# Feed-forward modulation of features 1024 to 2047 loaded beside gate and up chunks that start on half the features

## The chip, the cores and the metric

One core of a Trainium2 chip runs the whole program. The metric is device time in microseconds (us), from one launch, the smaller the better. TensorE (PE in the rows) does the matmuls and their weight loads (PEld), VectorE (DVE) and ScalarE (ACT) the element-wise work, SyncE (SP) issues every DMA of the kernel, GpSimd (POOL) is nearly unused. All inputs are float32. A product of two matrices is made of three matmuls in a rounded float32 format: each operand is split into a rounded part and a residue, and the product of the two residues is left out.

## The reference, cut to what matters

One encoder block over 256 tokens of 2048 features. A vector `c` gives six rows of 2048 numbers; two of them shift and scale the input of the mixer, two that of the feed-forward part, and two gate what is added to `x`.

```python
mod = (silu(c) @ ada_w + ada_b)                      # 2048 x 12288
shift_a, scale_a, gate_a, shift_f, scale_f, gate_f = split(mod, 6)
h = rmsnorm(x, norm1_w) * (1 + scale_a) + shift_a
proj = h @ w_in                                      # retention and attention heads
x = x + gate_a * (concat(retention, attention) @ w_o)
h = rmsnorm(x, norm2_w) * (1 + scale_f) + shift_f
ff = (silu(h @ w_gate) * (h @ w_up)) @ w_down        # 2048 -> 5632 -> 2048
x = x + gate_f * ff
return rmsnorm(x, final_norm_w)
```

## The kernel before

**Weights.** All weights lie in one stream in HBM, in the order in which they are used, and each is read once. A weight step loads 512 KB (two k-tiles of 128 features by 512 columns) into one of six staging buffers (`stg`). ScalarE casts it to the rounded part (`whi`, three buffers), VectorE subtracts to get the residue (`wlo`, three buffers), and TensorE does 12 matmuls of 512 columns for it: 2 k-tiles, 2 blocks of 128 tokens, 3 products. `run` walks a list of steps and keeps up to LOOK = 3 loads ahead of the step whose matmuls it records, except ahead of the steps named in URGENT.

**Modulation sets.** `ada_set` computes 512 columns of one of the six rows: eight loads of 512 KB (units), and at the end a spread that adds the bias. Units run in one of two ways. On TensorE a unit is four matmuls with the vector as a 32-column stationary operand (`c_pad`); four of them share the array side by side. On VectorE it is two multiply-adds of 128x512 into `ada_acc`. A 1 in a string of digits puts the set on TensorE. SC_F and SH_F are the scale and shift of the feed-forward part, GT_A and GT_F the two gates.

**Stages.** First the mixer's input projection, then attention and retention heads, the output projection, the norm of the new `x` (`norm_x2`), and the feed-forward part: eleven chunks of 512 columns of gate and up (`gate_up`), packed into the stationary layout by `pack`, and four chunks of `down`. Retention has, head by head, scores on TensorE (L615), a decayed copy on VectorE (`rP`, L618), an output on TensorE (L626), and statistics on VectorE; weight steps of `w_in` and `w_o` are filled in between by FILL_R. From attention on, the modulation sets GT_A, SC_F and SH_F are put between these steps at a rate set by ADA_RATE, in this order: four of GT_A, then SC_F and SH_F for features below K_LATE x 128 = 1536. By ADA_PE2 the second set of GT_A, the third of SC_F and the first of SH_F are on TensorE. One set of GT_F is on TensorE too, and fills the wait at the norm.

**Start of the feed-forward part.** The input of it (`h2`) is built two k-tiles at a time by `build_h2`. Chunks g0, u0 and g1 (gate 0, up 0, gate 1) first run over the six pairs of k-tiles below K_LATE, a weight step of each in turn: 18 weight steps. Beside each of them stands one unit of SC_F or SH_F for the last four k-tiles, 16 in all, on VectorE. Then the last k-tiles of `h2` are built and the three chunks are finished. The remaining three sets of GT_F follow on VectorE, one unit in every five weight steps.

The order in which each engine gets its instructions is set by a scheduler in the language layer, and each engine then runs its own list in that order. The lines that the steps below speak of are L122 (load), L124 (cast), L126 (residue), L132 to L134 (the three matmuls), L185 (load of a unit), L196 and L198 to L200 (a unit on TensorE and on VectorE), L222 (spread) and L728 (the norm's broadcast).

Of the kernel before, what the change touches and what calls it, by code (L numbers as in the profile page):

```python
# [8 lines left out]
F32 = mybir.dt.float32  # L9
# [32 lines left out]
LEAD = [1, 1, 3, 3, 3, 3, 3]  # L42
ADA_PE2 = "010000110000"
ADA_RATE = 0.8
# [41 lines left out]
def encoder_block(ctx: ExitStack, tc: tile.TileContext, x, cols, rows, pos, stream, out):  # L86
# [24 lines left out]
    c_act = const.tile([P, KT], F32, name="c_act")  # L111
    c_pad = const.tile([P, KT, 32], F32, name="c_pad")

# [59 lines left out]

    def ada_set(pool, sec, k0, nk, rowdst, on_pe):
        n = nk * P
# [4 lines left out]
        def acc_tile():  # L180
            return (pool or late["pool"]).tile([P, n], F32, name="ada_acc", tag="ada_acc", bufs=2 if pool else 1, padded_shape=[P, 512])

# [53 lines left out]

    def ada_stream(pool, sets):

        units, late = [], []
        for st in sets:  # L240
            loads, ends = ada_set(pool, *st)
# [10 lines left out]
    mid = mid_cm.__enter__()  # L252


# [115 lines left out]
    steps = [f(norm_x)]  # L370
    for u in ada_stream(mid, [(SC_A, *GROUPS[0], None, True), (SH_A, *GROUPS[0], None, True)]):
        steps += u
    steps += [f(turn_x, 0), f(build_h1, 0)]
    for gi, (k0, nk) in enumerate(GROUPS[:-1]):
        g0, gn_ = GROUPS[gi + 1]
        units = ada_stream(mid, [
            (sec, k, min(4, g0 + gn_ - k), None, ADA_PE[2 * gi + i] == "1") for k in range(g0, g0 + gn_, 4) for i, sec in enumerate((SC_A, SH_A))
# [290 lines left out]
    x2 = {}  # L668
    x2T = [pacc[n].rearrange("p b (k t) -> p (b k) t", t=T) for n in "vg"]

# [38 lines left out]

    def turn_x2(n):  # L710
        for g in range(2):
# [19 lines left out]
    h2 = {}  # L731

    def build_h2(k):
# [56 lines left out]
    early += [(sec, k, min(4, K_LATE - k), None) for sec in (SC_F, SH_F) for k in range(0, K_LATE, 4)]  # L790
    units = ada_stream(mid, [(*st, on == "1") for st, on in zip(early, ADA_PE2)])
    pe = dma = 0.0
# [17 lines left out]

    fill_f = [ada_set(mid, GT_F, 4 * i, 4, lambda: late["gate_f"], True) for i in range(N_FILL)]
    loads = [u for loads, _ in fill_f for u in loads]
    steps += [f(gate_f_tile)] + loads[:F_LEAD] + [f(turn_x2, 3)] + loads[F_LEAD:F_LEAD + F_MORE] + [f(norm_x2)] + loads[F_LEAD + F_MORE:]
    ends_f = [y for _, ends in fill_f for y in ends]


    def ffn_tiles():
        mid_cm.__exit__(None, None, None)
        late["pool"] = ctx.enter_context(tc.tile_pool(name="ffn", bufs=1))
        late["ap"] = late["pool"].tile([P, FT, 2 * T], F32R, name="ap")  # L820

    def sg_tile():
        late["sg"] = big.tile([P, 2, NB, CH], F32, name="sgs", tag="m8")

    def pack(j):
        for g in range(2):
            b = pairs(bank())
            ap = late["ap"]
# [3 lines left out]
            ks = slice(4 * j + 2 * g, 4 * j + 2 * g + 2)  # L832
            S.copy(ap[:, ks, 0:T], b)
            V.tensor_tensor(ap[:, ks, T:2 * T], b, ap[:, ks, 0:T].bitcast(F32), op=ALU.subtract)  # L834

    def gate_up(j, name, w):
        st = {}

        def body(kp, whi, wlo):
# [16 lines left out]
        return [("w", (w, kp, 2, j * CH, CH), lambda hi, lo, kp=kp: body(kp, hi, lo)) for kp in range(0, KT, 2)]  # L856

    units = ada_stream(None, [(GT_F, 4 * i, 4, lambda: late["gate_f"], False) for i in range(N_FILL, 4)])
    n_ch = DFF // CH
    g0, u0, g1, u1 = [gate_up(j, n, w) for j in range(2) for n, w in (("g", "w_gate"), ("u", "w_up"))]  # L860
    h_late = [(sec, K_LATE, KT - K_LATE, None) for sec in (SC_F, SH_F) if K_LATE < KT]
    units_h = ada_stream(mid, [(*st, on == "1") for st, on in zip(h_late, ADA_PE3)])
    steps.append(f(build_h2, 0))
    for kp in range(0, K_LATE, 2):
        if kp + 2 < K_LATE:
            steps.append(f(build_h2, kp + 2))
        for w in (g0, u0, g1):
            steps.append(w[kp // 2])
            if w is (g0, u0, g1)[F_END]:
                steps += ends_f  # L870
                ends_f = []
            for _ in range(H_RATE):
                if units_h:
                    steps += units_h.pop(0)
    for u in units_h:
        steps += u
    for k in range(K_LATE, KT, 2):
        steps.append(f(build_h2, k))
    steps += [f(ffn_tiles), f(sg_tile)]
    for w in (g0, u0, g1):  # L880
        steps += w[K_LATE // 2:]
    for j in range(1, n_ch):
        ws = u1 if j == 1 else gate_up(j, "g", "w_gate") + gate_up(j, "u", "w_up")
# [14 lines left out]
    def down(n):  # L898
# [14 lines left out]
        def body(kp, whi, wlo):  # L913
# [6 lines left out]
            for tb in range(NB):  # L920
                for q, hi, lo in st["w"]:
                    for i in range(2):
                        mm_tokens(st["o"][tb], late["ap"], q + i, tb, hi[:, i], lo[:, i], q + i == 0, q + i == FT - 1)
                if kp == FT - 2:
# [68 lines left out]
```

## Time and profile before

| | us |
|---|---|
| median of 3 runs | 1264.54 |
| lowest and highest run | 1262.27 and 1264.93 |
| the profiled execution, time | 1266.85 |
| the profiled execution, span of its core | 1264.9 |
| TensorE busy | 1224.4 |
| VectorE busy | 843.6 |
| ScalarE busy | 599.7 |
| bytes moved | 315.28 MB |

The span runs from the first to the last instruction of the core; the profiled execution's time is 1.95 us more than its span. Its mean granted TensorE clock is 0.992 of full speed. Matmul records overlap, since a matmul is recorded until its last result is out, so a TensorE that is busy the whole time may still not issue at its peak; the distance from one matmul's start to the next tells that.

### The profile page before, as it was taken

Reading aid. Unit: us, or ns where it says so; the run is one execution under the profiler, and the core shown is the slowest. Engines: PE = TensorE matmul, PEld = TensorE weight load, DVE = VectorE, ACT = ScalarE, POOL = GpSimd, SP = SyncE. Lnnn points to the kernel's source line nnn. Section 1 sums busy time; section 2 is a strip of 40 time slices with the busy share of each in tenths; the row PEclk is TensorE's granted clock in tenths of the full one; section 3 lists DMA queues with packets and bytes.
Section 4 is the critical chain, followed back from the end, with each engine's and each line's share of the span. In section 5 each row is a group of like instructions: output and inputs, shape, how many; then the busy total and the mean of one; then the engine's idle time right before and its main releaser. Section 6 shows DMA issues by size and latency. Waiting matters only on the chain.

```text
span 1264.9 us, 16232 instructions
## 1 busy us (share of the span) xinstructions
PE 1224.4 (97%) x6022; PEld 971.6 (77%) x6022; DVE 843.6 (67%) x1185; ACT 599.7 (47%) x811; POOL 1.7 (0%) x9
## 2 busy tenths in 40 slices
PE   5899899999999999899999999999999999999997
PEld 2676667788787788578888888888888888888885
DVE  2596988879997998886655556655654454554544
ACT  4552454645556665646344444444444434444433
POOL 0000000000000000000000000000000000000000
PEclk9999999999999999999999999999999999999998
DMA  8888898888877887897667657665765655555552
GB/s 337 321 301 309 276 317 299 290 311 290 298 255 289 306 301 278 299 349 250 211 220 233 201 183 274 222 203 202 275 219 188 226 187 194 190 198 190 192 196 88
DMA packets 88799, 315.28 MB, mean 249 GB/s; under 512 B 10248, under 2 KB 10376, under 8 KB 88208
## 3 DMA queue, kind: packets, MB, share of 16 engines
q1 hardware_dynamic: 88720, 314.24, 72.0%
q8 instruction: 47, 0.77, 0.3%
q14 instruction: 32, 0.26, 0.1%
HBM read 312.11 MB, written 2.10 MB: 248 GB/s over the span
## 4 chain that ended last, share of the span: by engine, by line
PE 85%; DVE 5%; DMA 5%; ACT 2%; issue 1%; SPq 0%; ACTq 0%; DVEq 0%
PE bank L133 25%; PE bank L134 25%; PE bank L132 25%; DMA stg<-in_stream 5%; DVE wlo L126 2%; PE bank L148 2%; PE bank L196 2%; DVE ada_acc L200 1%; ACT whi L124 1%; PE bank L514 1%; PE bank L138 1%; PE bank L513 1%; PE bank L626 1%; PE bank L615 1%; PE bank L140 1%
## 5 line engine op out<-in xcount | busy, mean ns | idle before, releaser
L126 DVE TENSOR_TENSOR wlo<-stg,whi 128x1024 fp32r<-128x1024 f32 (+2 forms) x400 | 478.7, 1198 | 341.2 <-ACT whi L124 339.6
L124 ACT CAST whi<-stg 128x1024 fp32r<-128x1024 f32 (+2 forms) x400 | 412.8, 1033 | 532.3 <-PE bank L134 417.2
L132 PE MATMUL bank<-whi,actt 128*128 128x512 f32 (+1 forms) x1184 | 457.9, 393 | 11.7 <-ACT whi L124 8.4
L133 PE MATMUL bank<-wlo,actt 128*128 128x512 f32 (+1 forms) x1184 | 461.7, 390 | 7.4 <-DVE wlo L126 7.0
L134 PE MATMUL bank<-whi,actt 128*128 128x512 f32 (+1 forms) x1184 | 459.2, 388 | 0.3 <-DVE actt L145 0.3
L132 PEld LDWEIGHTS bank<-whi,actt 128*128 128x128 f32 x1184 | 222.0, 189 | 64.9 <-ACT whi L124 12.7
L133 PEld LDWEIGHTS bank<-wlo,actt 128*128 128x128 f32 x1184 | 223.7, 189 | 62.4 <-DVE wlo L126 17.0
L134 PEld LDWEIGHTS bank<-whi,actt 128*128 128x128 f32 x1184 | 223.7, 189 | 44.9 <-DVE actt L145 1.1
L200 DVE SCALAR_TENSOR_TENSOR ada_acc<-stg,c_act,ada_acc 128x512 f32<-128x512 f32 (+1 forms) x240 | 175.0, 730 | 15.8 <-DMA stg<-in_stream 12.8
L132 PE MATMUL bank<-whi,ap 128*128 128x512 f32 x352 | 137.0, 389 | 0.0
L134 PE MATMUL bank<-whi,ap 128*128 128x512 f32 x352 | 136.9, 389 | 0.0
L133 PE MATMUL bank<-wlo,ap 128*128 128x512 f32 x352 | 136.9, 389 | 0.0
L133 PEld LDWEIGHTS bank<-wlo,ap 128*128 128x128 f32 x352 | 66.1, 188 | 13.8
L132 PEld LDWEIGHTS bank<-whi,ap 128*128 128x128 f32 x352 | 66.1, 188 | 13.8
L134 PEld LDWEIGHTS bank<-whi,ap 128*128 128x128 f32 x352 | 66.1, 188 | 13.5
L196 PE MATMUL bank<-stg,c_pad 128*32 128x256 f32 x544 | 48.0, 415 | 11.1 <-DMA stg<-in_stream 11.0
L196 PEld LDWEIGHTS bank<-stg,c_pad 128*32 128x32 f32 x544 | 13.0, 112 | 35.2 <-issue 26.0
L852 ACT ACTIVATE sgs<-bank 128x512 f32<-128x512 f32 x22 | 13.1, 597 | 10.5 <-PE bank L134 9.8
L145 DVE TENSOR_TENSOR actt<-hfull,actt 128x256 fp32r<-128x256 f32 x40 | 16.3, 420 | 2.2 <-ACT actt L144 2.1
L854 DVE TENSOR_TENSOR sgs<-bank,sgs 128x512 f32<-128x512 f32 x22 | 14.3, 682 | 0.6 <-PE bank L134 0.6
L834 DVE TENSOR_TENSOR ap<-bank,ap 128x512 fp32r<-128x512 f32 x22 | 14.1, 681 | 0.0
L226 DVE TENSOR_REDUCE mod<-bank 128x4 f32<-128x512 f32 (+3 forms) x18 | 8.0, 442 | 8.5 <-PE bank L222 8.3
(222 smaller groups left out, 711.1 us busy)
## 6 DMA issues: line engine op xcount, KB each, us to landing
stg<-in_stream SPq DMA_DIRECT2D x568, 512.0 KB, 4.4
stg<-in_stream SPq DMA_DIRECT2D x16, 288.0 KB, 4.1
stg<-in_stream SPq DMA_DIRECT2D x8, 384.0 KB, 2.8
xt<-in_x SPq DMA_DIRECT2D x2, 1024.0 KB
acc_cq<-in_x SPq DMA_DIRECT2D x8, 256.0 KB
out<-x SPq DMA_DIRECT2D x8, 256.0 KB, 2.9
acc_k<-in_rows SPq DMA_DIRECT2D x1, 1024.0 KB, 7.7
fw<-in_rows SPq DMA_DIRECT2D x1, 1024.0 KB
```

The costliest lines, as they stand in the source:

```text
L124: S.copy(hi, stg)
L126: V.tensor_tensor(lo, stg, hi.bitcast(F32), op=ALU.subtract)
L132: PE.matmul(o, lhsT=ah, rhs=whi, start=first, stop=False)
L133: PE.matmul(o, lhsT=ah, rhs=wlo, start=False, stop=False)
L134: PE.matmul(o, lhsT=al, rhs=whi, start=False, stop=last)
L145: V.tensor_tensor(dst[:, k, T:2 * T], tmp, dst[:, k, 0:T].bitcast(F32), op=ALU.subtract)
L148: PE.transpose(b[:, j, tb * P:(tb + 1) * P], src, ident)
L196: PE.matmul(a[q:q + 32, c:c + wide], lhsT=c_pad[:, k], rhs=w[:, j], start=c == 0 and k < 4, stop=c + wide == n and k >= KT - 4)
L200: V.scalar_tensor_tensor(out=a, in0=w[:, j], scalar=c_act[:, k:k + 1], in1=a, op0=ALU.mult, op1=ALU.add)
L834: V.tensor_tensor(ap[:, ks, T:2 * T], b, ap[:, ks, 0:T].bitcast(F32), op=ALU.subtract)
L852: S.activation(sg, o[tb], AF.Silu)
L854: V.tensor_tensor(sg, o[tb], sg, op=ALU.mult)
```

## The change

K_LATE goes from 12 to 8: the part of SC_F and SH_F that is ready ahead of the feed-forward part ends at feature 1024. Ahead of it stand 8 sets in place of 10, and of these only the second set of GT_A is on TensorE. The set that fills the wait at the norm is the third of SC_F (`h_late[0]`) in place of the first of GT_F. The other three late sets (24 units) run on VectorE beside the first 36 weight steps of the feed-forward part: g0, u0 and g1 over four pairs of k-tiles, and then gate chunks 2 to 7 over the same four pairs. Gates 1 to 7 leave PSUM after that half: ScalarE copies their two banks to SBUF (`spill`), and at the end of the second half VectorE adds the copy back. All four sets of GT_F follow on VectorE, one unit in every three weight steps.

Buffers move with it: the upper half of `x2T` and the temporary of `build_h2` (which now takes a `stg` buffer) leave the pool that is closed early, and `ap` becomes one tile for each chunk. The matmuls of a gate or up step go block by block instead of k-tile by k-tile; their number is the same.

```diff
-ADA_PE2 = "010000110000"
+ADA_PE2 = "01000000"
...
-N_FILL = 1
...
-K_LATE = 12
-ADA_PE3 = "00"
-H_RATE = 1
+K_LATE = 8
+N_SPILL = 7
...
     def build_h2(k):
...
-        V.tensor_tensor(v, v, rstd_b.unsqueeze(1).broadcast_to([P, 2, T]), op=ALU.mult)
+        if k < K_LATE:
+            scale_x2(k, 2)
         for j in range(2):
-            tmp = mid.tile([P, T], F32, name="hfull", tag="hfull", bufs=2)
+            tmp = wp.tile([P, T], F32, name="hfull", tag="stg", bufs=6)
...
-            if kp == 0:
+            if kp == 0 or (spilled and kp == K_LATE):
                 st["o"] = [bank() for _ in range(NB)]
             o = st["o"]
-            for i in range(2):
-                k = kp + i
-                for tb in range(NB):
-                    mm_tokens(o[tb], h2[k // 4], k % 4, tb, whi[:, i], wlo[:, i], k == 0, k == KT - 1)
+            for tb in range(NB):
+                for i in range(2):
+                    k = kp + i
...
-                if name == "g":
+                if name == "g" and (j, tb) in spills:
+                    V.tensor_tensor(sg, o[tb], spills.pop((j, tb)), op=ALU.add)
+                    S.activation(sg, sg, AF.Silu)
...
+        def spill(kp, whi, wlo):
+            body(kp, whi, wlo)
+            if kp < K_LATE - 2:
+                return
+            if j % 2:
+                spills["t"] = late["pool"].tile([P, 4, 2 * T], F32, name="spilled", tag="ap", bufs=n_ch)
+            for tb in range(NB):
+                d = spills["t"][:, 2 - 2 * (j % 2) + tb]
+                S.copy(d, st["o"][tb])
+                spills[j, tb] = d
...
+    def half_step(w):
+        nonlocal count
+        steps.append(w)
+        count += 1
+        if count % 4 and units_h:
+            steps.extend(units_h.pop(0))
...
+    for j in range(2, N_SPILL + 1):
+        for w in gs[j][:half]:
+            half_step(w)
     for u in units_h:
         steps += u
...
-            if i % 5 == 4 and units:
+            if i % 3 == 2 and units:
                 steps += units.pop(0)
```

The first place is retention on VectorE. Before, between two residues of `w_in` or `w_o` steps, only retention's own instructions stand there (`rP` the decayed scores, `bs` and `gnst` statistics, `dec` the decays):

```order
L618 SCALAR_TENSOR_TENSOR rP_3816<-bank_3813,dec_3809 128x256 x2
L629 BN_STATS bs_3835<-bank_3830 128x6
L629 BN_STATS bs_3838<-bank_3830 128x6
L630 BN_AGGR gnst_110<-bs_3835 128x2
L611 SCALAR_TENSOR_TENSOR dec_3872<-dist_108,lg_109,dec_3872 128x384
L630 BN_AGGR gnst_110<-bs_3838 128x2
L610 TENSOR_SCALAR dec_3928<-dist_108,lg_109 128x384
L611 SCALAR_TENSOR_TENSOR dec_3928<-dist_108,lg_109,dec_3928 128x384
L126 TENSOR_TENSOR wlo_3828<-stg_3824,whi_3826 128x1024
```

In the changed kernel, the piece that leads to a residue of the same stage:

```order
L627 BN_STATS bs_3766<-bank_3761 128x6
L616 SCALAR_TENSOR_TENSOR rP_3750<-bank_3747,dec_3743 128x256 x2
L628 BN_AGGR gnst_110<-bs_3766 128x2
L627 BN_STATS bs_3769<-bank_3761 128x6
L197 SCALAR_TENSOR_TENSOR ada_acc_3601<-stg_3709,c_act_80,ada_acc_3601 128x512
L628 BN_AGGR gnst_110<-bs_3769 128x2
L608 TENSOR_SCALAR dec_3793<-dist_108,lg_109 128x384
L609 SCALAR_TENSOR_TENSOR dec_3793<-dist_108,lg_109,dec_3793 128x384
L195 TENSOR_SCALAR ada_acc_3803<-stg_3741,c_act_80 128x512
L123 TENSOR_TENSOR wlo_3810<-stg_3806,whi_3808 128x1024
```

Multiply-adds into `ada_acc` of the two SH_F sets now stand on VectorE between retention's steps.

The second place is the same stretch on TensorE, where `rout` and `att` are turned and the scores (`qT`, `kT`) are made. Before:

```order
L148 MATMUL bank<-ident,rout 128x128 x8
L196 MATMUL bank<-stg,c_pad 32x256 x4
L148 MATMUL bank<-ident,att 128x128 x8
L196 MATMUL bank<-stg,c_pad 32x256 x4
L615 MATMUL bank<-qT,kT 128x256 x2
L196 MATMUL bank<-stg,c_pad 32x256 x4
L626 MATMUL bank<-acc_v,rP 128x128 x4
```

In the changed kernel:

```order
L145 MATMUL bank<-ident,rout 128x128 x8
L145 MATMUL bank<-ident,att 128x128 x8
L613 MATMUL bank<-qT,kT 128x256 x2
L624 MATMUL bank<-acc_v,rP 128x128 x4
L129 MATMUL bank<-whi,actt 128x512 x2
```

The units (`stg`, `c_pad`) are gone from TensorE there, and its other work follows directly.

The third place is SyncE's list of loads at the start of the feed-forward part, L122 a weight step and L185 a unit. Before:

```order
L122 DMA stg_4979<-in_stream 128x1024
L185 DMA stg_4997<-in_stream 128x1024
L122 DMA stg_5011<-in_stream 128x1024
L185 DMA stg_5019<-in_stream 128x1024
L122 DMA stg_5033<-in_stream 128x1024
L185 DMA stg_5041<-in_stream 128x1024
L122 DMA stg_5055<-in_stream 128x1024
```

In the changed kernel (L119 a weight step, L182 a unit):

```order
L119 DMA stg_5036<-in_stream 128x1024
L119 DMA stg_5044<-in_stream 128x1024
L182 DMA stg_5062<-in_stream 128x1024
L119 DMA stg_5067<-in_stream 128x1024
L182 DMA stg_5088<-in_stream 128x1024
L119 DMA stg_5104<-in_stream 128x1024
L182 DMA stg_5112<-in_stream 128x1024
```

Units and weight steps took turns; now there are three units to four weight steps, over 33 weight steps in place of 16.

## Rows read from the trace of the kernel before

**Rows 1.** The page: busy time by engine, and the chain that ended last.

```profile
PE 1224.4 (97%) x6022; PEld 971.6 (77%) x6022; DVE 843.6 (67%) x1185; ACT 599.7 (47%) x811; POOL 1.7 (0%) x9
PE 85%; DVE 5%; DMA 5%; ACT 2%; issue 1%; SPq 0%; ACTq 0%; DVEq 0%
```

**Rows 2.** Busy time of the engines by stretch, columns as in the first line.

```profile
core 0: us, PE busy (x) PEld busy (x) DVE busy (x) ACT busy (x) POOL busy (x), PEclk, DMA share, GB/s
377.70:417.60 39.90, 39.90 (x277) 28.31 (x277) 31.77 (x85) 26.64 (x50) 0.00 (x0) 1.00 0.75 277
417.60:454.40 36.80, 36.80 (x202) 29.62 (x202) 34.71 (x67) 22.84 (x38) 0.00 (x0) 1.00 0.89 318
...
545.00:571.00 26.00, 25.26 (x111) 19.76 (x110) 22.80 (x30) 9.95 (x11) 0.00 (x0) 1.00 0.96 356
```

**Rows 3.** TensorE in order of time, retention: start, duration, line, count, idle before.

```profile
385.25 1.07 PE L196 MATMUL bank<-stg,c_pad 128*32 128x256 f32 x16
386.25 1.13 PE L615 MATMUL bank<-qT,kT 128*128 128x256 f32 x4
...
388.77 0.66 PE L222 MATMUL bank<-ident,ada_acc 128*128 128x128 f32 x4
389.26 1.04 PE L148 MATMUL bank<-ident,att 128*128 128x128 f32 x8
390.23 0.64 PE L196 MATMUL bank<-stg,c_pad 128*32 128x256 f32 x8
390.80 1.09 PE L148 MATMUL bank<-ident,rout 128*128 128x128 f32 x8
```

**Rows 4.** VectorE in order of time, retention.

```profile
377.69 0.15 DVE L558 TENSOR_REDUCE stat<-stat 128x2 f32<-128x4 f32 x1
...
404.81 0.62 DVE L611 SCALAR_TENSOR_TENSOR dec<-dist,lg,dec 128x384 f32<-128x384 f32 x1
...
416.43 1.22 DVE L126 TENSOR_TENSOR wlo<-stg,whi 128x1024 fp32r<-128x1024 f32 x1
...
434.93 0.74 DVE L200 SCALAR_TENSOR_TENSOR ada_acc<-stg,c_act,ada_acc 128x512 f32<-128x512 f32 x1
435.59 0.17 DVE L226 TENSOR_REDUCE mod<-bank 128x4 f32<-128x16 f32 x1
```

**Rows 5.** TensorE in order of time, a weight step of retention and the start of the feed-forward part.

```profile
421.58 0.39 PE L133 MATMUL bank<-wlo,actt 128*128 128x512 f32 x1
...
512.04 0.71 PE L728 MATMUL bank<-dg,ones 128*128 128x128 f32 x4
...
516.01 0.73 PE L132 MATMUL bank<-whi,actt 128*128 128x512 f32 x2 [2.68 <-ACT whi L124]
...
524.75 1.10 PE L218 MATMUL bank<-ada_acc,ones 128*128 128x512 f32 x2 [0.17 <-DVE ada_acc L212]
```

**Rows 6.** Granted clock, the column behind POOL, in two stretches of 1 us.

```profile
518.00:519.00 1.00, 1.00 (x3) 0.81 (x4) 1.00 (x4) 1.00 (x2) 0.00 (x0) 0.50 1.04 426
521.00:522.00 1.00, 1.00 (x6) 0.81 (x5) 1.00 (x2) 1.00 (x2) 0.00 (x0) 1.00 0.31 61
```

**Rows 7.** TensorE in order of time, `down`.

```profile
1248.73 0.39 PE L132 MATMUL bank<-whi,ap 128*128 128x512 f32 x1
...
1255.31 0.39 PE L134 MATMUL bank<-whi,ap 128*128 128x512 f32 x1
```

**Rows 8.** The turns of `pack`: count, shortest, median, longest ns, first and last start.

```profile
L148 PE MATMUL bank<-ident,sgs x88: 270/272/273, 598.1 to 1021.5; 128*128 128x128 f32 x88
```

**Rows 9.** ScalarE's longest wait, 516 to 571 us: total, times, longest one.

```profile
ACT whi L124 <- DMA stg<-in_stream: 21.0, 13, 3.0
```

**Rows 10.** SyncE's longest wait, 500 to 700 us.

```profile
SPq L122 <- DVE wlo L126: 81.9, 50, 3.2
```

**Rows 11.** The page, groups: evacuations of a PSUM bank on ScalarE and VectorE.

```profile
L852 ACT ACTIVATE sgs<-bank 128x512 f32<-128x512 f32 x22 | 13.1, 597 | 10.5 <-PE bank L134 9.8
L854 DVE TENSOR_TENSOR sgs<-bank,sgs 128x512 f32<-128x512 f32 x22 | 14.3, 682 | 0.6 <-PE bank L134 0.6
```

More of the change, by code (lines that the diff above doesn't have):

```diff
@@ L171, in encoder_block, with ada_set @@
     late = {}
[L174 removed]
+    def ada_set(sec, k0, nk, rowdst, on_pe):
         n = nk * P
@@ L180, in acc_tile @@
         def acc_tile():
-            return (pool or late["pool"]).tile([P, n], F32, name="ada_acc", tag="ada_acc", bufs=2 if pool else 1, padded_shape=[P, 512])
+            return wp.tile([P, n], F32, name="ada_acc", tag="ada_acc", bufs=2, padded_shape=[P, 512])
         def load(c, t):
@@ L235, in ada_set, with ada_stream @@
         return loads, [f(finish), f(spread)]
-    def ada_stream(pool, sets):
+    def ada_stream(sets):
         units, late = [], []
         for st in sets:
-            loads, ends = ada_set(pool, *st)
+            loads, ends = ada_set(*st)
             for u in loads:
@@ L370, in encoder_block @@
     steps = [f(norm_x)]
-    for u in ada_stream(mid, [(SC_A, *GROUPS[0], None, True), (SH_A, *GROUPS[0], None, True)]):
+    for u in ada_stream([(SC_A, *GROUPS[0], None, True), (SH_A, *GROUPS[0], None, True)]):
         steps += u
@@ L668, in encoder_block @@
     x2 = {}
-    x2T = [pacc[n].rearrange("p b (k t) -> p (b k) t", t=T) for n in "vg"]
+    x2T = {0: pacc["v"].rearrange("p b (k t) -> p (b k) t", t=T)}
     def out_proj(k0):
@@ L790, in encoder_block @@
     early += [(sec, k, min(4, K_LATE - k), None) for sec in (SC_F, SH_F) for k in range(0, K_LATE, 4)]
-    units = ada_stream(mid, [(*st, on == "1") for st, on in zip(early, ADA_PE2)])
+    units = ada_stream([(*st, on == "1") for st, on in zip(early, ADA_PE2)])
     pe = dma = 0.0
@@ L809, in gate_f_tile @@
         late["gate_f"] = big.tile([P, D], F32, name="gate_f", tag="m8")
[L811 to L814, printed above, removed]
+    h_late = [(sec, k, 4, None) for k in range(K_LATE, KT, 4) for sec in (SC_F, SH_F)]
+    loads, ends_h = ada_set(*h_late[0], True)
+    loads = [[u] for u in loads]
+    for i, g in enumerate((f(turn_x2, 3), f(norm_x2))):
+        for u in loads[:(F_LEAD, F_MORE)[i]]:
+            steps += u
+        loads = loads[(F_LEAD, F_MORE)[i]:]
+        steps.append(g)
+    for u in loads:
+        steps += u
     def ffn_tiles():
@@ L819, in ffn_tiles @@
         late["pool"] = ctx.enter_context(tc.tile_pool(name="ffn", bufs=1))
-        late["ap"] = late["pool"].tile([P, FT, 2 * T], F32R, name="ap")
+        late["ap"] = {}
     def sg_tile():
@@ L825, in pack @@
     def pack(j):
+        ap = late["ap"][j] = late["pool"].tile([P, 4, 2 * T], F32R, name="ap", tag="ap", bufs=n_ch)
         for g in range(2):
             b = pairs(bank())
-            ap = late["ap"]
             for i in range(2):
@@ L837, in gate_up @@
         st = {}
+        spilled = name == "g" and 1 <= j <= N_SPILL
         def body(kp, whi, wlo):
-            if kp == 0:
+            if kp == 0 or (spilled and kp == K_LATE):
                 st["o"] = [bank() for _ in range(NB)]
             o = st["o"]
-            for i in range(2):
-                k = kp + i
-                for tb in range(NB):
-                    mm_tokens(o[tb], h2[k // 4], k % 4, tb, whi[:, i], wlo[:, i], k == 0, k == KT - 1)
+            for tb in range(NB):
+                for i in range(2):
+                    k = kp + i
+                    first, last = k == 0 or (spilled and k == K_LATE), k == KT - 1 or (spilled and k == K_LATE - 1)
+                    mm_tokens(o[tb], h2[k // 4], k % 4, tb, whi[:, i], wlo[:, i], first, last)
             if kp < KT - 2:
@@ L854, in body, with step @@
                     V.tensor_tensor(sg, o[tb], sg, op=ALU.mult)
-        return [("w", (w, kp, 2, j * CH, CH), lambda hi, lo, kp=kp: body(kp, hi, lo)) for kp in range(0, KT, 2)]
-    units = ada_stream(None, [(GT_F, 4 * i, 4, lambda: late["gate_f"], False) for i in range(N_FILL, 4)])
+        def spill(kp, whi, wlo):
[8 more added lines that the diff above has]
+                spills[j, tb] = d
+        def step(kp):
+            fn = spill if spilled and kp < K_LATE else body
+            return ("w", (w, kp, 2, j * CH, CH), lambda hi, lo: fn(kp, hi, lo))
+        return [step(kp) for kp in range(0, KT, 2)]
+    spills = {}
+    units = ada_stream([(GT_F, 4 * i, 4, lambda: late["gate_f"], False) for i in range(4)])
     n_ch = DFF // CH
-    g0, u0, g1, u1 = [gate_up(j, n, w) for j in range(2) for n, w in (("g", "w_gate"), ("u", "w_up"))]
-    h_late = [(sec, K_LATE, KT - K_LATE, None) for sec in (SC_F, SH_F) if K_LATE < KT]
-    units_h = ada_stream(mid, [(*st, on == "1") for st, on in zip(h_late, ADA_PE3)])
+    gs, us = [[gate_up(j, n, w) for j in range(n_ch)] for n, w in (("g", "w_gate"), ("u", "w_up"))]
+    units_h = ada_stream([(*st, False) for st in h_late[1:]])
+    half = K_LATE // 2
     steps.append(f(build_h2, 0))
+    count = 0
+    def half_step(w):
[4 more added lines that the diff above has]
+            steps.extend(units_h.pop(0))
     for kp in range(0, K_LATE, 2):
@@ L866, in encoder_block @@
             steps.append(f(build_h2, kp + 2))
[L867 to L874, printed above, removed]
+        for w in (gs[0], us[0], gs[1]):
+            half_step(w[kp // 2])
+        if kp == 0:
+            steps += ends_h
+            ends_h = []
+        if kp == K_LATE - 4:
+            steps += [f(scale_x2, K_LATE, 4), f(scale_x2, K_LATE + 4, 4), f(ffn_tiles), f(sg_tile)]
+    for j in range(2, N_SPILL + 1):
+        for w in gs[j][:half]:
+            half_step(w)
     for u in units_h:
         steps += u
[L877 to L881, printed above, removed]
+    steps += [f(build_h2, k) for k in range(K_LATE, K_LATE + 4, 2)]
+    steps += gs[0][half:half + 2] + [f(build_h2, k) for k in range(K_LATE + 4, KT, 2)] + gs[0][half + 2:] + us[0][half:]
+    steps.append(f(gate_f_tile))
     for j in range(1, n_ch):
-        ws = u1 if j == 1 else gate_up(j, "g", "w_gate") + gate_up(j, "u", "w_up")
+        ws = (gs[j][half:] if j <= N_SPILL else gs[j]) + us[j]
         for i, w in enumerate(ws):
```

14 lines of the change are left out of this document (10 added, 4 removed).

## The prediction

> **What bounds the kernel now.** I read the page first: TensorE is busy for 1224.4 us of the span, and 85% of the chain that ended last runs on it [rows 1]. So what counts is TensorE's issue time and the places where it waits. In the feed-forward part one matmul follows another after 0.227 us (29 starts in 6.58 us) [rows 7], which makes a weight step of 12 matmuls 2.72 us. The busy time by stretch says more than the totals: in 377.7 to 417.6 us, retention, TensorE is busy throughout, VectorE for 31.8 of 39.9 us; in the next 36.8 us VectorE is busy for 34.7 us; in 545 to 571 us, the start of the feed-forward part, the DMA share is 0.96 [rows 2]. Elsewhere after 598 us VectorE has room. TensorE, VectorE and the loads are thus each close to full somewhere, and a saving on one is worth only what the others leave of it.
>
> **Retention: what leaves TensorE.** Two sets leave it, 16 units. Two units in a row take 1.0 us from start to next start, one unit 0.57 us [rows 3], so they cost 1.0 + 14 x 0.57 = 9.0 us. Two spreads (0.49 us each [rows 3]) move to the feed-forward part with their sets. By TensorE's rows alone the mixer would end 10.0 us earlier.
>
> **Retention: what VectorE gets.** The number of sets on VectorE ahead of the feed-forward part is seven before and after, but not their place. Sets are taken at the same rate in the same order. Where units 49 to 64 stood on TensorE (SC_F 3 and SH_F 1) there now stand SH_F 1 and SH_F 2 on VectorE; units 65 to 80, VectorE's last ones, are gone. So VectorE's two sets are not added, they come some 50 us earlier, into the stretch in which it also has retention's copies and statistics. I count to a fixed point: the sixth residue after 377.7 us, which ends at 417.6 us [rows 4]. Up to it the changed order has 26 more operations into `ada_acc`; one takes 0.66 us to the next start [rows 4], 17.2 us in all. Four decay operations less stand ahead of it, the longer kind 0.6 us [rows 4], some 1.7 us. VectorE's 31.8 us of work becomes 31.8 + 17.2 - 1.7 = 47.3 us, so that residue is ready at 377.7 + 47.3 = 425.0 us at the earliest. TensorE took it at 421.6 us [rows 5]; without the 14 units that stood ahead (1.0 + 12 x 0.57 = 7.8 us) it asks for it at 413.8 us. It waits 11.2 us, spread over the six steps. What is queued behind on TensorE is everything, weight steps and scores alike. From there to the norm's broadcast at 512.0 us [rows 5] it has 90.4 us, less two units (1.1) and two spreads (1.0): 88.3 us. The broadcast comes at 425.0 + 88.3 = 513.3 us in place of 512.0: **+1.3 us** if VectorE never waits. It waited 39.9 - 31.8 = 8.1 us in this stretch, for TensorE, and rather more for ScalarE's casts and exponentials; with other work to do in between, I keep 1 us of that, and the whole for the range. Where VectorE loses its last two sets, after 440 us, nothing is gained: TensorE was the full engine there already.
>
> **The norm.** The filler is one TensorE set in both (SC_F 3 for GT_F 1), so no time changes. Both kernels start the feed-forward part through the same chain: TensorE idles for 2.7 us before 516.0 us [rows 5], and its granted clock is then at the lower level, 0.50 from 518 us, and 1.00 again from 521 us [rows 6]. This stays.
>
> **The start of the feed-forward part.** From the broadcast to the first turn of `pack` TensorE has 27 weight steps (73.5 us), the broadcast and the last unit (1.3), one spread of a gate (0.9) and two others (1.0): 76.7 us, which ends at 588.7; the turn starts at 598.1 us [rows 8]. So 9.4 us are lost there. Some 5.9 of them are lost by the third weight step: the gate's spread, after 24 matmuls, should start at 518.8 and starts at 524.75 us [rows 5]. The other 3.5 us are lost while 34 loads go beside 18 weight steps: at the 356 GB/s of the stretch [rows 2] a load of 512 KB takes 1.47 us, so 1.89 loads per step take 2.78 us against TensorE's 2.72, and ScalarE waits 21.0 us for loads [rows 9]. After the change it is 24 units beside 33 steps, 1.73 loads, 2.54 us. VectorE has a residue, 1.2 us, and 0.73 times two operations of 0.74 us [rows 4], 2.3 us per step. Both are then below 2.72 us, and I let 2 of the 3.5 us go. Against that stand 1.0 us for the two spreads that moved here: **-1.0 us**.
>
> **Edits that I cost at nothing.** Fourteen evacuations to SBUF on ScalarE (0.6 us each [rows 11]) and fourteen additions on VectorE (0.7 us [rows 11]) are covered, because a chunk's banks are wanted again only after the next chunk's four steps, 10.9 us; without that cover they would cost 14 x 0.6 = 8.4 us. GT_F's rate of one unit in three steps needs 1.33 x 1.47 = 2.0 us of loads for 2.72 us of TensorE. The temporaries of `build_h2` now take staging buffers: SyncE already waits 81.9 us for such buffers [rows 10], and a temporary holds one for a cast and a subtraction, about a microsecond. Eight of them fall into the first 12 steps; if each delays the loads by its whole time that is up to 8 us, if the loads have room by then nothing; I take nothing, since the loads now need 93% of the time. The order of matmuls, block by block, is that of `down`, whose distance is 0.227 us.
>
> **Sum.** Mixer +1.3 + 1.0, feed-forward part -1.0: +1.3 us on the profiled execution's 1266.85, 1268.2. The median lies 2.3 us below that execution, so 1265.9 us.
>
> **Two rules of the Trainium skill.** The row shows the clock at 0.50 after a stretch in which TensorE did hardly anything [rows 6]. The Trainium skill, page TensorE: Matmul & The Clock Gate, section HAM oscillation, warns of just this: waits between bursts of matmuls let the clock fall. By that rule the new waits in retention could cost on top; by the rows they would not, while VectorE is late anyway. The Trainium skill, page DMA: Bandwidth & Descriptors, section Bandwidth, gives some 358 GB/s for a core's share of HBM; the trace agrees where the loads are full (356 at a share of 0.96 [rows 2]), and the sum by either is the same.
>
> **The rivals.**
> *Slower: VectorE's waits in retention stay.* If all 8.1 us of waiting remain between the longer work, the broadcast comes at 521.4 us, and the sum is +8.4, 1273 us; half of them give 1269. From 2.2 us of waiting on, the kernel is slower by over 0.2%. For it speaks that exponentials and casts on ScalarE (26.6 us busy there [rows 2]) answer VectorE in turn; against it that a part of what VectorE waited for was TensorE, which is now early, and that the new operations wait for a load alone.
> A clock that falls in those waits belongs to it: from 518 to 521 us 12 matmuls cost twice the time, some 2 us for each fall that comes after VectorE has caught up.
> *Faster: VectorE is not what ends last.* If half of the 11.2 us of waiting does not occur, because the six steps are less strictly behind the units than I count, the mixer gains 4 to 5 us, and if the whole 3.5 us at the start go too, the sum is some -6: 1258 us. For it speaks that TensorE really has 10.0 us less to do; against it that VectorE's list is run in order.
> *The halves do not hold.* If the copies or the staging buffers get into TensorE's way, up to 8 us: 1274 us.
>
> **How the numbers follow.** No measurable change (within 0.2%, 2.5 us, about what a measurement of this kernel can tell) has 0.38, slower 0.35 (of it 0.07 for the halves), faster 0.27. The range goes from 1258 to 1273 us: the faster rival at its lower end, the slower one at its upper end. The likeliest case alone spans 1262 to 1267.
>
> **What would show it.** In the changed profile VectorE should be busy for nearly all of 378 to 425 us, with TensorE waiting there for residues (`wlo`) for some 10 us in all, and the norm's broadcast should start between 512 and 516 us. The first half steps should run at 2.72 us each from about the eighth on, with a DMA share around 0.9, and no wait of TensorE for a copy to SBUF. The prediction is wrong if the broadcast starts before 509 us, if VectorE idles in retention for more than 4 us, or if the 33 steps beside the late sets take over 95 us.

## The result and the profile after

The changed kernel takes 1276.54 us, the median of 4 runs (1273.64 to 1282.29), where the kernel before took 1264.74 us beside it. The ratio is 1.010 with a 95% interval of 1.0083 to 1.0118: some 12 us slower, where 1265.9 us was forecast. The profiled execution is the quickest of the four, 1273.64 us with a span of 1271.8 us; it stands against the 1264.9 us of the span before.

The page: busy time by engine, and the chain that ended last.

```profile
PE 1218.5 (96%) x5894; PEld 969.9 (76%) x5894; DVE 868.3 (68%) x1229; ACT 605.7 (48%) x823; POOL 1.7 (0%) x9
PE 64%; DMA 15%; DVE 14%; issue 5%; ACT 2%; SPq 0%; DVEq 0%; ACTq 0%
```

TensorE has 6 us less to do than in [rows 1], but its share of the chain falls from 85 to 64%: VectorE takes 14% of it in place of 5, and DMA 15% in place of 5. Something waits for loads that did not before.

To find where, I cut both executions at the same events: the first score of retention, the norm's broadcast, and the first and the last turn of `pack` (its matmuls with the identity, which turn a finished chunk). TensorE in order of time, first the score of the kernel before, then score and broadcast of the changed one:

```profile
383.42 1.02 PE L615 MATMUL bank<-qT,kT 128*128 128x256 f32 x4
```

```profile
378.75 1.02 PE L613 MATMUL bank<-qT,kT 128*128 128x256 f32 x4
...
510.24 0.71 PE L728 MATMUL bank<-dg,ones 128*128 128x128 f32 x4
```

The turns of `pack` of the changed kernel, which answer to [rows 8] (count, durations, first and last start):

```profile
L145 PE MATMUL bank<-ident,sgs x88: 271/273/273, 649.0 to 1028.4; 128*128 128x128 f32 x88
```

| stretch, us | before | after | difference | forecast |
|---|---|---|---|---|
| start to first score | 383.4 | 378.8 | -4.7 | 0 |
| first score to broadcast | 128.6 | 131.5 | +2.9 | +2.3 |
| broadcast to last turn of `pack` | 509.5 | 518.2 | +8.7 | -1.0 |
| last turn to the end of the span | 243.4 | 243.4 | 0 | 0 |

The first line is no effect of the change: no engine's order of instructions differs before 373.8 us, TensorE's 1301st matmul starts at 254.1 us where it started at 258.6, and the runs below show the first score anywhere from 378.7 to 383.4 us. The second is nearly as forecast: the five executions with this order in retention (this one, `gate4`, `no_add`, `touch` and `behind` below) take 131.1 to 132.9 us for it, the two of the kernel before 128.6. The third is the surprise, and the waits of VectorE show it. This is the changed kernel, 640 to 960 us, while GT_F's units run (total, times, longest one):

```profile
DVE ada_acc L197 <- DMA stg<-in_stream: 71.6, 27, 5.0
DVE wlo L123 <- ACT whi L121: 33.9, 29, 1.5
DVE ada_acc L195 <- DMA stg<-in_stream: 10.8, 3, 4.8
```

VectorE stands still for 82.4 us in 30 waits for the load of a unit, 2.7 us each. TensorE waits there for what is queued behind; its matmuls, and its weight loads (these overlap the matmuls, so the two do not add up):

```profile
PE bank L130 <- DVE wlo L123: 5.2, 8, 1.1
```

```profile
PEld bank L130 <- DVE wlo L123: 11.4, 15, 1.5
```

In these 320 us TensorE runs 1399 matmuls, and 1442 in `behind` below, where VectorE no longer waits for units: 43 fewer, which at 0.227 us each are 9.8 us.

The rows of one such wait, in order of time (VectorE, ScalarE and SyncE's DMA queue, SPq):

```profile
748.30 1.22 DVE L123 TENSOR_TENSOR wlo<-stg,whi 128x1024 fp32r<-128x1024 f32 x1
...
749.55 0.33 SPq L182 DMA_DIRECT2D stg<-in_stream  x1
750.21 1.23 DVE L123 TENSOR_TENSOR wlo<-stg,whi 128x1024 fp32r<-128x1024 f32 x1 [0.69 <-ACT whi L121]
...
751.85 1.05 ACT L121 CAST whi<-stg 128x1024 fp32r<-128x1024 f32 x1 [1.67 <-PE bank L131]
...
755.03 0.75 DVE L197 SCALAR_TENSOR_TENSOR ada_acc<-stg,c_act,ada_acc 128x512 f32<-128x512 f32 x1 [3.60 <-DMA stg<-in_stream]
...
755.70 1.22 DVE L123 TENSOR_TENSOR wlo<-stg,whi 128x1024 fp32r<-128x1024 f32 x1
```

The residue at 748.30 ends at 749.52 and frees a staging buffer; at 749.55 SyncE issues the unit's load into it. VectorE does one more residue and starts the unit's multiply 5.5 us after that issue; for the last 3.6 of them it waits for the load. The cast at 751.85 is done at 752.90, yet its residue starts at 755.70, behind the multiply. The waits for ScalarE (0.69 us) and for matmuls (1.67 us) in these rows are shorter and end before it does, and the loads have room: the DMA share of 640 to 960 us is 0.67.

Of VectorE's list the Trainium skill says the same in its page PSUM — Partial Sum Buffer, section Engine vs sequencer instructions: the queues of ScalarE, VectorE and GpSimd are strict FIFO. The trace agrees: a residue whose inputs are there stands 2.8 us behind a multiply whose input is not.

### The profile page after: what moved, and what is told of

The parts are those of the page before. It is cut to its first block, busy times and chain, and to the rows that moved or that the text cites. A ratio compares the mean times of both kernels' runs of the same rounds, so it can differ in the third digit from the quotient of the medians.

```text
span 1271.8 us, 16066 instructions
## 1 busy us (share of the span) xinstructions
PE 1218.5 (96%) x5894; PEld 969.9 (76%) x5894; DVE 868.3 (68%) x1229; ACT 605.7 (48%) x823; POOL 1.7 (0%) x9
## 4 chain that ended last, share of the span: by engine, by line
PE 64%; DMA 15%; DVE 14%; issue 5%; ACT 2%; SPq 0%; DVEq 0%; ACTq 0%
PE bank L130 19%; PE bank L131 19%; PE bank L129 18%; DMA stg<-in_stream 15%; DVE wlo L123 6%; DVE ada_acc L197 4%; PE bank L193 2%; PE bank L145 2%; ACT whi L121 1%; PE bank L512 1%; PE bank L135 1%; PE bank L511 1%; DVE ap L845 1%; PE bank L137 1%; PE bank L136 1%
## 5 line engine op out<-in xcount | busy, mean ns | idle before, releaser
L197 DVE SCALAR_TENSOR_TENSOR ada_acc<-stg,c_act,ada_acc 128x512 f32<-128x512 f32 (+1 forms) x270 | 197.6, 733 | 76.5 <-DMA stg<-in_stream 74.1
L193 PE MATMUL bank<-stg,c_pad 128*32 128x256 f32 x416 | 37.3, 417 | 11.8 <-DMA stg<-in_stream 11.7
L193 PEld LDWEIGHTS bank<-stg,c_pad 128*32 128x32 f32 x416 | 10.3, 112 | 30.7 <-issue 22.4
L195 DVE TENSOR_SCALAR ada_acc<-stg,c_act 128x512 f32<-128x512 f32 (+1 forms) x18 | 8.6, 476 | 11.6 <-DMA stg<-in_stream 11.6
L881 ACT COPY spilled<-bank 128x512 f32<-128x512 f32 x14 | 8.2, 585 | 14.9 <-PE bank L131 14.9
L867 ACT ACTIVATE sgs<-sgs 128x512 f32<-128x512 f32 x14 | 8.5, 632 | 13.9 <-DVE sgs L866 13.9
```

What stands on the lines that cost most here:

```text
L193: PE.matmul(a[q:q + 32, c:c + wide], lhsT=c_pad[:, k], rhs=w[:, j], start=c == 0 and k < 4, stop=c + wide == n and k >= KT - 4)
L197: V.scalar_tensor_tensor(out=a, in0=w[:, j], scalar=c_act[:, k:k + 1], in1=a, op0=ALU.mult, op1=ALU.add)
```

## The experiments

Three theories stood at first. Theory 1: VectorE waits in order for units at one in three steps, and residues come late. Theory 2: the copies to SBUF, the additions of the spilled half and the silu behind them. Theory 3: the loads' rate. "First to last turn" below is from the first to the last start in the row of `pack`'s turns, 379.4 us in the changed kernel (the expectations count to the start of the last group of turns, some 0.8 us less).

**One unit in four steps (`gate4`).**

```diff
-            if i % 3 == 2 and units:
+            if i % 4 == 3 and units:
```

> GT_F's units come after every fourth weight step instead of every third; the 32 units then last until chunk 10. Theory 1 (VectorE waits in order for a unit's load, which SyncE could issue only when a staging buffer came free, and the residues behind it come late to TensorE): the change lost 9.6 us between the first and the last turn of pack, 0.3 us for each of the 32 units at one in three steps, and the kernel before nothing at one in five; at one in four a third to a half of the loss should remain, 3 to 5 us, so 1270 to 1272 us, with VectorE's waits for loads at L197 well below the 76.5 us of the change. Theory 2 (the copies to SBUF, the additions and silu behind them): the number of those is the same, 1276 us. Theory 3 (the loads' rate itself): 1.25 loads per step against 1.33, 6% less, so at most a small part comes back, 1275 us.

Measured: 1268.51 us, ratio to the kernel before 1.0024 (1.0012 to 1.0037). Turns of `pack`, and VectorE's waits for units from 590 to 1040 us:

```profile
L145 PE MATMUL bank<-ident,sgs x88: 271/272/273, 654.3 to 1024.0; 128*128 128x128 f32 x88
```

```profile
DVE ada_acc L197 <- DMA stg<-in_stream: 29.5, 25, 2.0
```

First to last turn is 369.7 us, 9.7 less than in the changed kernel, and the work in it is the same (all 32 units). More came back than theory 1 asked for, and theories 2 and 3 fall: neither the copies nor the additions had gone, and the loads per step had hardly changed.

**The kernel before at one unit in three (`before_gate3`).**

```diff
-            if i % 5 == 4 and units:
+            if i % 3 == 2 and units:
```

> The kernel before with one edit: its 24 units of GT_F after every third weight step instead of every fifth. No half chunks, no copies, no additions. Theory 1: 24 units x 0.3 us, 7 us slower than the kernel before, 1270 to 1273 us, with VectorE waiting for staging loads in 600 to 800 us as in the change. Theory 2: no loss, 1264 to 1265 us.

Measured: 1265.15 us, ratio 1.0003 (0.9991 to 1.0015); first to last turn 423.4 us (595.0 to 1018.4), as in [rows 8]. Theory 1 missed by some 5 us: a rate close to that of the change (5 units in 16 steps against 4 in 12) costs this kernel nothing. VectorE waits for units here too, but little:

```profile
DVE ada_acc L200 <- DMA stg<-in_stream: 18.8, 12, 3.4
```

**Without the additions (`no_add`).** The first half's sum is left out of seven chunks of gate.

```diff
-                if name == "g" and (j, tb) in spills:
-                    V.tensor_tensor(sg, o[tb], spills.pop((j, tb)), op=ALU.add)
-                    S.activation(sg, sg, AF.Silu)
-                elif name == "g":
+                if name == "g":
```

> The change without the addition of the spilled half: silu reads the bank of the second half alone, so the first half of the features is left out of seven chunks of gate; copies to SBUF, loads, units and matmuls stay. Theory 2 (the chain bank, addition, silu holds the banks or VectorE): most of the 9.6 us comes back, 1267 to 1269 us. Theory 1: VectorE has 14 operations of 0.7 us less, but still waits for the units' loads: 1274 to 1276 us.

Measured: 1273.85 us (1.0067, 1.0047 to 1.0087); first to last turn 376.1 us, and 64.8 us of waits of VectorE for units. Two thirds of the loss or more stay, so the additions are not the cause. Whether the 3.3 us that went are due to the 14 operations is not shown: `shf1_alone` below, with all of them, takes 376.4 us for the same stretch.

**The units' loads without VectorE's work (`touch`).** GT_F is not computed.

```diff
+            if sec == GT_F:
+                if t == 0:
+                    G.memset(a, 0.0)
+                G.tensor_copy(out=a[:, 0:8], in_=w[:, 0, 0:8])
+                return
```

> The change with GT_F's work on VectorE left out: every load of its 32 units is still issued at its place into the same ring of six buffers, but a copy of eight elements per partition on GpSimd, which has nothing else to do, takes it in place of VectorE's two operations (the gate of the feed-forward part is then not computed). Theory 1: nothing in VectorE's list waits for a unit's load any more, so the 9.6 us come back: 1266 to 1268 us. Theory 3 (the loads, their number or their buffers): they are all there, 1274 to 1277 us. Theory 2: 1275 to 1277 us.

Measured: 1267.88 us (1.0024, 1.0007 to 1.0040); first to last turn 369.7 us (653.1 to 1022.8). Loads and buffers are there, at the same rate, and the loss is gone once nothing in VectorE's list waits for them. This run also takes the units' 64 multiplies off VectorE, so it does not yet tell waiting from work; the next one does.

**A new theory.** Rate alone does not do it, VectorE's waits do. Reading the order of the instructions of both kernels, I found the difference in the place of the units. A load goes into the staging buffer of the sixth load before it; in the changed kernel a unit's first multiply stands 0 to 2 rows behind the residue that frees this buffer, for all but one of the 31 units that I followed. VectorE thus reaches it while the load, 4.7 us from issue to landing in the median of all, has only begun. In the kernel before at one in three it is 0 to 19 rows: 12 or more for 10 of the 24 units, 6 or fewer for the others, and why these others, the first eight in a row among them, cost nothing is open. At one in four it is 0 rows for most units, and yet nothing is lost: VectorE waits 1.1 us per unit there (34.3 us, with L195's 4.8, for 32 units), and TensorE has four steps, 10.9 us, to cover it.

The test (`behind`) moves the units in VectorE's list alone:

```diff
-        V.tensor_tensor(lo, stg, hi.bitcast(F32), op=ALU.subtract)
+        los.append(V.tensor_tensor(lo, stg, hi.bitcast(F32), op=ALU.subtract))
...
+    def behind(fn, *args):
+        with tc.issue_after(los[-2].ins): return fn(*args)
...
-lambda w, c=c, t=t: body(c, t, w)
+lambda w, c=c, t=t: behind(body, c, t, w) if sec == GT_F else body(c, t, w)
```

> The change with one edit: each of GT_F's units on VectorE is placed behind the residue of the weight tile two steps ahead. Rate (one unit in three steps), loads, their order on SyncE, ScalarE's and TensorE's orders are the same row for row; only VectorE's list differs between the first and the last turn of pack. The first four runs changed the theory: a rate of one in three alone did not slow the kernel before (1265.2), one in four brought the change to 1268.5, and the orders show why: in the change a unit's first multiply stands 0 to 2 rows behind the residue whose staging buffer its load takes, so that VectorE waits for nearly the whole load each time. Theory 1b (the place in VectorE's list): the 9.7 us between first and last turn of pack go, from 378.6 us to 369 us, 1266 to 1268 us, and VectorE's waits for loads at L197, 72 us between 590 and 1040 us, fall below 15 us. Rival 1a (the rate with six buffers: a unit that is taken later holds its buffer longer, and the loads behind it come later): 1273 us or more.

Measured: 1268.24 us, ratio 1.0024 (1.0014 to 1.0034), 8.3 us below the change. Turns of `pack`, then VectorE's waits from 640 to 960 us:

```profile
L145 PE MATMUL bank<-ident,sgs x88: 270/272/273, 653.4 to 1023.1; 128*128 128x128 f32 x88
```

```profile
DVE wlo L123 <- ACT whi L121: 100.8, 77, 2.4
DVE ada_acc L209 <- DMA bias_row<-in_rows: 1.9, 3, 0.9
```

First to last turn is 369.7 us again, and no wait for a unit is left, with all the work in place. In time, a stretch that answers to the one above:

```profile
753.47 1.23 DVE L123 TENSOR_TENSOR wlo<-stg,whi 128x1024 fp32r<-128x1024 f32 x1 [1.50 <-ACT whi L121]
754.62 1.53 DVE L197 SCALAR_TENSOR_TENSOR ada_acc<-stg,c_act,ada_acc 128x512 f32<-128x512 f32 x2
...
755.12 1.05 ACT L121 CAST whi<-stg 128x1024 fp32r<-128x1024 f32 x1 [1.68 <-PE bank L131]
...
756.18 0.33 SPq L182 DMA_DIRECT2D stg<-in_stream  x1
756.20 1.23 DVE L123 TENSOR_TENSOR wlo<-stg,whi 128x1024 fp32r<-128x1024 f32 x1
```

The unit's two multiplies start at once, and the residue follows its cast within 0.1 us. Orders on TensorE, ScalarE and SyncE, the rate and the loads are those of the change: theory 1b stands, and rival 1a (buffers held longer make the loads late) falls. What `behind` still takes more than the kernel before (1265.43 us beside it) is 2.8 us, about what retention takes more (131.6 against 128.6 us).

**The mixer.** The first of the two SH_F sets goes back to TensorE (`behind_shf1`), then both (`behind_shf2`); the edit for the first:

```diff
-ADA_PE2 = "01000000"
+ADA_PE2 = "01000010"
```

> As the run before, and the first of the two SH_F sets of the mixer, 8 units, goes back from VectorE to TensorE. Mixer theory (VectorE is what ends last in retention): TensorE gets 8 x 0.57 = 4.6 us more, VectorE 16 x 0.66 = 10.6 us less; the sixth residue would be ready 10 us earlier and TensorE asks 4.6 us later, so of its 11.2 us of waiting nothing is left, and from the first score to the norm's broadcast it takes 126 to 128 us in place of the change's 131.5: 3 to 5 us less than the run before, 1262 to 1264 us. Rival (TensorE's own list is what ends last, the change's 131.5 us came from elsewhere): 4 to 5 us more than the run before.

> As the run before, with both SH_F sets of the mixer on TensorE, as the kernel before had two sets there. Mixer theory: VectorE was no longer what ends last with one set moved, so the second costs TensorE its 4.6 us: 3 to 5 us more than with one set, 1266 to 1268 us. Rival (VectorE still is what ends last with one set there): again 2 us less or more.

Measured: with one set 1261.25 us, ratio 0.9962 (0.9949 to 0.9975); with both 1264.98 us, 0.9991 (0.9979 to 1.0004). From first score to broadcast it is 128.0 and 127.9 us; in `behind` it was 131.6. For one set the stretch agrees with the mixer theory, and the median is 0.7 us below the expected range. For both, the median is 3.7 us above that with one set, as expected, but by these two traces none of it lies in this stretch. Busy time and granted clock, with one set and with both (columns as in [rows 2]):

```profile
425.00:430.00 5.00, 5.00 (x23) 4.20 (x22) 4.60 (x7) 1.55 (x3) 0.00 (x0) 0.73 0.74 252
```

```profile
377.70:425.00 47.30, 47.30 (x324) 33.40 (x323) 38.35 (x95) 33.19 (x59) 0.00 (x0) 1.00 0.78 281
```

With both, TensorE has no wait there and the full clock. With one it waits 2.0 us for a spread, and then runs at a granted clock of 0.73 for 5 us. These take back most of what the units give: 4.6 us less work, against 2.0 us of waiting and some 1.4 us of low clock (0.27 of 5 us).

The same kernel with one set once more (`shf1_again`), since 3.8 of the 8.3 us that its trace gained on `behind` (7.0 in the medians) lay ahead of the first score:

> The same kernel as behind_shf1, once more: its median lay 7 us below that of the run without the SH_F set on TensorE, but its trace shows 3.6 us of that in retention and 3.8 us before the first score, where both kernels issue the same instructions in the same order. If the start only differs from run to run, the first score comes near 382.5 us this time and the median near 1264 us; if the start is part of the kernel, 378.8 us and 1261 us again.

Measured: 1262.65 us, ratio 0.9978 (0.9963 to 0.9994); first score at 378.7 us, broadcast at 503.9 us, 125.2 us between. The early start came again, but the median fell between the two expectations. The start differs between executions of kernels that issue the same there; what sets it, and whether this kernel meets the early one more often, is open. In retention this execution is 2.8 us shorter than the other one of the same kernel, with a wait of 1.8 us at the same spread and the clock at 1.00 behind it:

```profile
PE bank L219 <- DVE ada_acc L197: 1.8, 1, 1.8
```

```profile
425.00:430.00 5.00, 5.00 (x28) 4.31 (x27) 5.00 (x10) 3.22 (x4) 0.00 (x0) 1.00 0.78 273
```

Against this run both sets on TensorE cost 2.6 us of the stretch (127.9 against 125.2) and 2.3 us in the median, so what the second set costs there differs with the execution that it is compared with.

**The set on TensorE alone** (`shf1_alone`), without the edit to VectorE's list:

> The change with the one SH_F set back on TensorE and nothing else; GT_F's units stay where the change has them in VectorE's list. The two causes are in different stretches, so they should add: from the first score to the broadcast 128.0 us as in the last runs (131.5 in the change), from the first to the last turn of pack still 378 us: 3 to 7 us less than the change, 1270 to 1273 us. Rival (they are one cause, VectorE being late in retention carries over into the feed-forward part): from the first to the last turn of pack below 373 us.

Measured: 1269.71 us, ratio 1.0047 (1.0031 to 1.0064), 6.8 us below the change. First score to broadcast is 127.6 us, first to last turn 376.4 us where 379.4 were. The rival asked for less than 373 us and falls: the two causes are apart. The 3 us between these two numbers may be a difference between executions; nothing was repeated to tell.

**Spreads later (`shf1_delay4`).** In the mixer, four units between a set's last unit on VectorE and its spread, in place of two:

```diff
-    def ada_stream(sets):
+    def ada_stream(sets, dve_delay=DVE_DELAY):
...
-            late.append((PE_DELAY if st[-1] else DVE_DELAY, ends))
+            late.append((PE_DELAY if st[-1] else dve_delay, ends))
...
-    units = ada_stream([(*st, on == "1") for st, on in zip(early, ADA_PE2)])
+    units = ada_stream([(*st, on == "1") for st, on in zip(early, ADA_PE2)], 4)
```

> As shf1_again, and the finish and the spread of a set on VectorE in the mixer come four units later instead of two. In behind_shf1 TensorE waits 2.0 us in retention for such a spread (L219 at 424.4 us, for ada_acc), with the clock at 0.73 in the 5 us after. If that wait is the whole, 2 to 4 us less than shf1_again, and from the first score to the broadcast 124 to 126 us; rival (the accumulator is then held longer and the next set's units wait for it on VectorE, or TensorE waits for a residue in its place): within 1 us of shf1_again or more.

Measured: 1260.44 us, ratio 0.9960 (0.9945 to 0.9976). First score to broadcast is 123.7 us (382.5 to 506.2), below what I expected, and TensorE's longest wait from 377 to 506 us is this:

```profile
PE bank L130 <- DVE wlo L123: 0.5, 1, 0.5
```

This kernel, with the units behind, one SH_F set on TensorE and the spreads later, is faster than both the kernel before (by 5 us) and the change (by 16 us). Its median is 2.2 us below that of `shf1_again` and 0.8 us below that of `behind_shf1`, which is the same kernel, with ranges that overlap: the last edit's own part in the time is not shown by the medians. The trace shows that the wait for the spread is gone.

## Why the prediction was wrong, step by step

**GT_F's rate: the step that failed.** The prediction put this edit among those that cost nothing: one unit in three steps needs 2.0 us of loads for 2.72 us of TensorE. That number was right, with the DMA share at 0.7, and beside the point. A throughput says that the loads fit; it doesn't say when a load can be issued, nor who stands behind it in VectorE's list. The load can go only when a buffer comes free, and the unit's multiply stood right behind the residue that frees it. The cost was 9.7 us by the traces, nearly all of the 10.6 us by which 1276.5 us lies above the forecast of 1265.9 us. By the medians of `gate4`, `touch` and `behind` it was 8.0 to 8.7 us, and in `shf1_alone`, the second execution with the same list there, 6.7 us by the trace (376.4 against 369.7). Two things had to come together: the place in the list (`behind` takes it away) and a rate that leaves no time to make up for it (`gate4` takes that away). The prediction looked at SyncE's waits for buffers [rows 10] and asked only what `build_h2`'s temporaries would do with them, not what the units would. The kernel became slower, as one of the rivals said, but that rival's mechanism was retention; its sign was luck.

**Retention: the bound right, its path in part.** +2.3 us was forecast, +2.9 measured. VectorE was to be busy for nearly all of 378 to 425 us, and TensorE to wait some 10 us. Busy time in that stretch, then TensorE's waits from 377 to 506 us, of the changed kernel:

```profile
377.70:425.00 47.30, 39.70 (x192) 32.35 (x191) 44.89 (x98) 25.05 (x43) 0.00 (x0) 0.89 0.75 244
```

```profile
PE bank L130 <- DVE wlo L123: 4.3, 3, 1.8
PE bank L129 <- ACT whi L121: 3.2, 1, 3.2
PE bank L219 <- DVE ada_acc L197: 1.5, 1, 1.5
```

VectorE idles for 2.4 us (4 was the bound), and TensorE waits 9.0 us. But only 4.3 of these are for residues, as was forecast, and the longest single wait is for a cast whose load came late:

```profile
389.41 1.22 DVE L123 TENSOR_TENSOR wlo<-stg,whi 128x1024 fp32r<-128x1024 f32 x1
...
390.70 0.33 SPq L119 DMA_DIRECT2D stg<-in_stream  x1
...
395.33 1.04 ACT L121 CAST whi<-stg 128x1024 fp32r<-128x1024 f32 x1 [1.84 <-DMA stg<-in_stream]
...
396.43 0.50 PE L129 MATMUL bank<-whi,actt 128*128 128x512 f32 x1 [3.22 <-ACT whi L121]
```

SyncE issues the load when VectorE's residue ends (390.63), and the cast starts 4.6 us later. So VectorE sets the pace here by two ways: its residues, and the buffers that it frees late, the same way that cost the time in the feed-forward part. The broadcast came at 510.2 us, below the 512 to 516 forecast, because the execution was 4.7 us early from the start; counted from the first score it is where it should be. Moving one set back confirmed the direction: with less for VectorE the stretch was shorter, though TensorE had more to do. That taking two sets from TensorE gains nothing while VectorE is the later one was right for the right reason.

**The clock.** In the changed kernel's retention the mean clock is 0.89, where it was 1.00 in [rows 2]: it is 0.50 from 398 to 402 us, behind the wait of 3.2 us. The prediction held such a fall to cost nothing while VectorE is late anyway. What it cost there no run separates; two executions of `behind_shf1`'s kernel, with and without a fall behind nearly the same wait, differ by 2.8 us in the stretch. The price of some 2 us for each fall was read too high: from 518 to 521 us the matmuls of the kernel before start 0.43 us apart, so that seven fit there and not twelve, and such a fall costs some 1.4 us. The Trainium skill, page TensorE: Matmul & The Clock Gate, section HAM oscillation, says that waits between bursts of matmuls let the clock fall; the trace agrees, with 0.50 behind the 3.2 us.

**The start of the feed-forward part: right.** From the broadcast to the first turn stand 47 weight steps (127.8 us), the broadcast and the last unit (1.3), and four spreads (2.0), 131.1 us; the turn came 138.8 us after the broadcast, so 7.7 us are lost where 9.4 were, and 7.4 were forecast. The DMA share of 516 to 600 us is 0.90. One sign that the prediction named for being wrong did appear: the 33 steps take 96.2 us (514.2 to 610.4), over its 95. But its own terms, 33 x 2.72, three spreads and 4.7 us (the 7.4 less the 2.7 ahead of the first step), add up to 96, so that sign was set below its sum. And the 356 GB/s that it took for full loads is a mean of that stretch and no ceiling: [rows 6] has 426 GB/s in 1 us.

**Copies, additions, temporaries: right.** The fourteen copies run from 550.8 to 620.8 us, and TensorE waits for none of them: from 512 to 652 us it waits 4.5 us in all, the last time at 527.5 us. `behind` has all fourteen copies and additions too, and TensorE waits for nothing from 640 to 960 us. The rival in which the halves do not hold named staging buffers and 1274 us, close to what came by luck: its mechanism was the halves, and these did hold; the buffers got in the way through the units of GT_F.

## What to carry to other kernels

When a change raises the rate at which loads are used, compare more than bytes with time: follow one load from the event that frees its buffer to the instruction that uses it, and count what stands between them on the engine that waits. If it is less than the landing time of a load, that engine stands still at each of them, with all that is queued behind; whether that costs time depends on what the others have to cover it (in `gate4` it cost nothing). An operation that can wait is put behind those that TensorE needs next, by an explicit order if a scheduler sets the list; and work goes to an engine by what is left of it in that stretch, not over the whole span.

## What the runs showed of the hardware

- The first 380 us of the program differ by up to 4.7 us between executions of kernels that issue the same instructions there (first score at 378.7 to 383.4 us). A difference of medians of 3 us could not be read without cutting the traces at common events.
- Waits of TensorE of 1.8 and 2.0 us at the same place of the same kernel were followed by a granted clock of 1.00 in one execution and 0.73 over 5 us in the other, the two levels being 1.00 and 0.50 [rows 6]. The stretch from first score to broadcast took 125.2 and 128.0 us. In the changed kernel a wait of 1.8 us for a residue, up to 419.7 us, was followed by 0.50 from 422 to 424 us, so the length of the wait alone does not tell.
- The four runs of the changed kernel lie 8.6 us apart, the 12 runs of `behind` 4.6 us. VectorE's waits for units are not needed for such a spread: the 12 runs of `touch`, which has none, lie 9.9 us apart, and those of `shf1_again` 8.6. What sets it is open.
